# Two layers with attention, recurrence and a convolution: the z gates as plain float32 products queued behind the scores, the modulation split into single steps

## Chip, cores and metric

One NeuronCore of a Trainium2 chip runs the whole program. The metric is the device time of one execution in microseconds (us), the median of several runs. In the text PE is TensorE, DVE VectorE, ACT ScalarE, POOL GpSimd and SP the queue that issues most loads.

## What is computed

256 tokens of width 1024 pass two equal layers ("first block"), then one block of latent attention and a matrix LSTM, and then a layer of experts (256 gathers of rows). The change lies in the two layers, and in the modulation vectors that the second block uses. Cut to that, the reference is:

```python
for l in range(2):
    h = rms_norm(x, norm_g[l])
    proj = h @ w_in[l]
    (q, k_c, v_c, k_s, v_s, k_w, v_w, g_lin, z_nsa, u_lru, z_lru, glu_a, glu_b, z_conv) = split(proj)
    ...
    y_nsa = nsa_attention(...)      # compressed, selected and window branch
    y_lru = rg_lru(u_lru, ...)      # linear recurrence over the tokens
    y_conv = conformer_conv(...)    # 31 taps, layer norm, product with w_pw2
    mixed = concatenate([y_nsa * silu(z_nsa), y_lru * silu(z_lru), y_conv * silu(z_conv)])
    x = x + mixed @ w_out[l]

mod_lat = silu(c) @ w_ada + b_ada       # second block: shifts, scales and gates
mod_ctx = silu(c_ctx) @ w_ada + b_ada
```

The z gates are 12 of the 128-wide column blocks of the first product. The modulation is a product of two vectors with a 1024 x 6144 matrix; its sixth part is summed elsewhere and stays.

## The kernel before

Tokens lie along the free dimension (256), features along the 128 partitions. A weight tile is 128 x 1024 float32 (512 KB): eight 128 x 128 blocks that make 128 output features. `wload` (L310) issues its load on SP into one of five raw buffers, `wsplit` (L318) makes a high part of it on ACT (copy to the reduced type fp32r) and a low part on DVE (the difference), and `mm3` (L350) multiplies with three products a block: high by high, low by high, high by low, 24 products of 256 columns for a tile. The normalised input is held split in the same way (`hh`, `hl`).

A layer runs: norm, products of the column blocks (`proj2`, L572), attention (`attend`, L764) with other work between its steps, and the out-projection (`woa`, 8 tiles; `wob`, 4 tiles). `attend` yields after each score: 14 pieces per layer (for two blocks of 128 queries, the selected and window branches and then the compressed one). The string ORDER (L237) says what is put after each yield: letters A to F are pairs of z tiles (`zpair`, L755), digits the gates of the recurrence, c the compression of keys, s the scan, w, p, q the product behind the convolution, x, y, z its norm. `conv_norm` starts with a sum over the four convolution outputs (the first product of line 412 in the tail), and the taps of the convolution are DVE instructions that are put in behind splits.

A list scheduler orders the instructions on each engine: `at(us)` gives what follows a priority, loads and splits get an earlier one, and `tc.issue_after(ins)` puts an instruction behind another on its engine. So a z pair stands where its priority puts it, and its tiles fill the time between scores.

The modulation (`modulation`, `part`, L958) has five parts of eight tiles, each tile with four small products (32 x 256) of line 963 into one PSUM buffer `c`, from two raw buffers (`wm`). `hook` (L1665) calls three parts in layer 0 and two in layer 1, at fixed priorities P["mt"]. A "step" below is one tile with its four products.

```python
def zpair(i):
    acc = proj2(20 + i)
    th = mk(b1, [128, 2, T], tag="tmp2", bufs=2)
```

Of the kernel before, what the change touches and what calls it, by code (L numbers as in the profile page):

```python
# [9 lines left out]
F32R = mybir.dt.float32r  # L10
# [219 lines left out]

P = dict(np=5, glu=14, kv=35, kk=40, q=41, cmp=46, cmpd=5, w1n=62, cv0=32, cvd=35, att=57, attd=5, mix=137, woa=131, ln=145, pw2=160, wob=138, mod=5, ll=25000, sl=6000, nm=3, mt=(62, 80, 170, 243, 270), sp=29, L0=10, L1=196, S=369, B=500, cx=125, h1=2, h2=6, X=16, lri=37, lnk=7, tp=2, tq=0, ta=0, ml=40, mld=2.6, rt=36, g0=-32, ga=104, gb=161, gc=157)

# [4 lines left out]
def program(tc, A, dbg=lambda *a: None, stop=99):  # L241
# [11 lines left out]
        return p.tile(list(shape), dt, name=f"{tag}_{cnt[0]}", tag=tag, **kw)  # L253

    def mm(out, lhsT, rhs, start, stop):
        pe.matmul(out, lhsT, rhs, start=start, stop=stop)  # L256

    def tr(out, in_, ident):
        pe.transpose(out, in_, ident)  # L259
# [90 lines left out]
    def mm3(out, pairs, first=True, last=True, late=False):  # L350

        n = len(pairs)
        for i, (ah, al, bh, bl) in enumerate(pairs):
            mm(out, ah, bh, first and i == 0, False)
            if late:
                mm(out, al, bh, False, False)
            else:
                mm(out, ah, bl, False, False)
                mm(out, al, bh, False, last and i == n - 1)
        if late:  # L360
            for i, (ah, al, bh, bl) in enumerate(pairs):
                mm(out, ah, bl, False, last and i == n - 1)

    def rsqrt(p, v, shape, tag, bufs=2):

# [20 lines left out]
    def psum(tag, shape):  # L386
        if tag == "acc":
            turn[1] = (turn[1] + 1) % 3
            tag = "acx" if turn[1] == 0 else "acc"
        return mk(ps, shape, tag=tag, bufs=PB[tag])  # L390
# [55 lines left out]
    hh = mk(cp, [128, 8, T], F32R, tag="hh")  # L446
    hl = mk(cp, [128, 8, T], F32R, tag="hl")

    def norm_apply(p, src, gain, shift=None, hi=None, lo=None, bc=None):
        if bc is None:  # L450
            bc = norm_rstd(p, [src[:, k] for k in range(8)], D)
        g6 = None if hi is not None else slot("g6", 2048).rearrange("p (k t) -> p k t", k=8)
        if hi is None:
            hi, lo = hh, hl
        p0 = tc.cur_priority
        for k in range(0, 8, 2):
            tc.cur_priority = p0
            t = mk(p, [128, 2, T], tag="tmp2", bufs=2) if g6 is None else g6[:, k:k + 2]
            for q in range(2):
                scaled[:] = [dve.scalar_tensor_tensor(t[:, q], src[:, k + q], gain[:, k + q:k + q + 1], bc, op0=mul, op1=mul)]  # L460
            if shift is None:
                last = act.activation(hi[:, k:k + 2], t, AF.Copy)
                if g6 is not None:
                    tc.cur_priority = p0 + 4000
                tt(lo[:, k:k + 2], t, hi[:, k:k + 2].bitcast(F32), sub)
            else:
                for q in range(k, k + 2):
                    last = act.activation(hi[:, q], t[:, q - k], AF.Identity, bias=shift[:, q:q + 1])  # L468
                if g6 is not None:
                    tc.cur_priority = p0 + 4000  # L470
                for q in range(k, k + 2):
                    stt(lo[:, q], t[:, q - k], shift[:, q:q + 1], hi[:, q].bitcast(F32), add, sub)
        tc.cur_priority = p0
        return last
# [5 lines left out]
    def slot(tag, n, dt=F32, bufs=1):  # L480

        return mk(b1, [128, SLOTS[tag]], dt, tag=tag, bufs=bufs)[:, 0:n]
# [80 lines left out]
    def layer(l, L, hook=lambda n: None):  # L563
# [8 lines left out]
        def proj2(i, t=None):  # L572

            acc = psum("acc", [128, 2, T])
            for q in range(2):
                if t is not None:
                    at(L + t + 2.6 * q)
                wh, wl = wsplit(A["w1"][l, i + q], [128, 8, 128])
                mm3(acc[:, q], [(wh[:, k], wl[:, k], hh[:, k], hl[:, k]) for k in range(8)], late=i == 0)
            if t is not None:  # L580
                at(L + t + 5.2)
            return acc
# [170 lines left out]
        gzc = slot("gz4", 1024).rearrange("p (i t) -> p i t", i=4)  # L753

        def zpair(i):  # L755
            acc = proj2(20 + i)
            th = mk(b1, [128, 2, T], tag="tmp2", bufs=2)
            act.activation(th, acc, AF.Tanh, scale=0.5)
            stt(gz[:, i:i + 2] if i < 8 else gzc[:, i - 8:i - 6], th, 1.0, acc, add, mul)


        onat = []

        def attend(b):  # L764
            bs = slice(b * 128, b * 128 + 128)
# [13 lines left out]
            for bi in (1, 2):  # L779
                step = 2 - b  # L780
                for jj in range(0, 4, step):
                    js = list(range(jj, jj + step))
                    sps = psum("s", [128, step, 2, nk])
                    for ji, j in enumerate(js):
                        mm(sps[:, ji], qT[:, j, bs], kz[:, bi - 1, :, 0:nk], True, False)
                        mm(sps[:, ji, :, nk - 128:], identb, cmaskb[:, None, :].broadcast_to([128, 2, 128]), False, True)
                    nh = 2 * step
                    s2 = sps.rearrange("p a g k -> p (a g) k")
                    mx = mk(b1, [128, 4], tag="mxs", bufs=4)
# [23 lines left out]

            cps = psum("s", [128, 4, 2, 15])
            for j in range(4):
                mm(cps[:, j], qT[:, j, bs], kcz, True, True)
            c8 = cps.rearrange("p j g n -> p (j g) n")
            sc = mk(b1, [128, 8, 15], tag="sc", bufs=1)
            cm = C("cmpm")[:, 16 * b:16 * b + 15]
# [21 lines left out]
            onat.append(oT)  # L841


        g6 = slot("g6", 2048, F32R).rearrange("p (w i t) -> p w i t", w=2, i=4)
        mch, mcl = g6[:, 0], g6[:, 1]

        def pick(i):
            return (hh, hl, i) if i < 8 else (mch, mcl, i - 8)

        def msplit(i, src):  # L850
            h, lo, j = pick(i)
# [42 lines left out]
                     q=lambda: conv_proj(2, pw))  # L894
        for i in range(4):
            steps[str(i)] = lambda i=i: lru_gates(i)
        for i, c in enumerate("ABCDEF"):
            steps[c] = lambda i=i: zpair(2 * i)
        for c in "xyz":
            steps[c] = lambda: next(cn)  # L900
        order = ORDER[l].split(",")
# [18 lines left out]
        for n in range(0, 8, 2):  # L920
            acc = psum("acc", [128, 2, T])
            for q in range(2):
                at(L + P["woa"] + 2.6 * (n + q))
                wh, wl = wsplit(A["woa"][l, n + q], [128, 8, 128])
                mm3(acc[:, q], [(wh[:, k], wl[:, k], hh[:, k], hl[:, k]) for k in (4, 5, 6, 7, 0, 1, 2, 3)])
            stt(XT[:, n:n + 2], acc, 0.5, XT[:, n:n + 2], mul, add)
            for c in order.pop(0):
                steps[c]()

        for n2 in range(4):  # L930
            at(L + P["wob"] + 2.6 * n2)
            wh, wl = wsplit(A["wob"][l, n2], [128, 4, 256])
            acc = psum("acc", [128, 2, T])
            for q in range(2):
                s = slice(q * 128, q * 128 + 128)
                mm3(acc[:, q], [(wh[:, k, s], wl[:, k, s], mch[:, k], mcl[:, k]) for k in range(4)])
            stt(XT[:, n2 * 2:n2 * 2 + 2], acc, 0.5, XT[:, n2 * 2:n2 * 2 + 2], mul, add)
# [6 lines left out]
    def modulation():  # L944
# [3 lines left out]
        def prep():  # L948
# [6 lines left out]
            ts(s2, s2, 0.5, None, mul)  # L955
            act.activation(sc0, sc[:, :, 0], AF.Copy)

        def part(m):  # L958
            acc = psum("c", [128, 256])
            for k in range(8):  # L960
                w = wload(A["wada"][m, k], [128, 4, 256], "wm", NWM, b1)
                for j in range(4):
                    pe.matmul(acc[32 * j:32 * j + 32], sc[:, k], w[:, j], start=k == 0, stop=k == 7,  # L963
                              tile_position=(0, 32 * j))
            rows = slot("ang", 256)
            act.activation(rows, acc, AF.Copy)
            tp = psum("c", [128, 2, 128])
            for q in range(2):
                tr(tp[:, q], rows[:, q * 128:q * 128 + 128], ident)
            src = tp.rearrange("p q (j w) -> p j q w", w=32)[:, :, :, 0:2]  # L970
            tt(modt[:, m * 8:m * 8 + 8].rearrange("p (j q) w -> p j q w", q=2), src,
               P2("bada")[:, m * 8:m * 8 + 8].rearrange("p (j q) -> p j q", q=2)[:, :, :, None].broadcast_to([128, 4, 2, 2]), add)
            if m == 1:
                for nm, w in (("lat", 0), ("ctx", 1)):
                    mg[nm] = mk(cp, [128, 8], tag="mg" + nm)
                    stt(mg[nm], modt[:, 8:16, w], 1.0, P2("g1"), add, mul)
            if m == 4:
                mg["pr"] = mk(cp, [128, 8], tag="mgpr")
                stt(mg["pr"], modt[:, 32:40, 0], 1.0, P2("g2"), add, mul)

        return [prep] + [lambda m=m: part(m) for m in (1, 0, 2, 4, 3)[:int(P["np"])]]

    def modsum(acc, m, k):

# [5 lines left out]
            stt(acc, w, s, acc, mul, add)  # L990

    def modparts():
        for m in (4, 3)[int(P["np"]) - 3:]:
            acc = mk(b1, [128, 1024], tag="wm", bufs=NWM)
            for k in range(8):
                modsum(acc, m, k)
# [661 lines left out]
            pass  # L1658
        pp.release()

    steps = modulation()
    at(P["mod"])
    steps.pop(0)()

    def hook(n, l):  # L1665
        if n == 0:
            if l == 1:
                next(two)
            return
        for i in range(min(int(P["nm"]), len(steps)) if l == 0 else len(steps)):  # L1670
            at(P["mt"][int(P["np"]) - len(steps)])
            steps.pop(0)()

    layer(0, P["L0"], lambda n: hook(n, 0))
    two = second(P["L1"] + P["cx"], P["S"])
# [18 lines left out]
```

## Time and profile before

| | |
|---|---|
| median of 3 runs | 1381.29 us (1377.42 to 1384.13) |
| the profiled execution | 1384.02 us |
| its span in the trace | 1382.2 us |
| mean granted clock of TensorE | 0.946 |
| PE, DVE, ACT busy | 1193.9, 991.6, 530.5 us |
| float32 weight splits, DVE | 142 in 171.4 us |
| gathers of the experts, chain | 27% of the span |

A row of the trace gives the start (us from the span's start), the busy time, the engine, the line of the kernel, the operation with the tile it writes and the tiles it reads, and in brackets how long the engine had been idle and what ended that. A float32 product of 128 or more columns is two hardware instructions, so that x4 is two products of the program; a split product is one. Layer 0 takes the time from about 16 to 248 us, layer 1 from there to about 500.

### The profile page before, as it was taken

The numbers are of one execution on the slowest core, as the hardware profiler recorded it, in microseconds if no ns is written. First come the engines' busy times: TensorE is split into PE (matmuls) and PEld (weight loads), VectorE is DVE, ScalarE is ACT, GpSimd is POOL, SyncE is SP. The second block draws the span as 40 slices with busy tenths as digits, with TensorE's granted clock in tenths as the row PEclk, the third lists the DMA queues.
The fourth block names the chain that finished last, engine by engine and source line by source line (L and its number), as shares of the span: only waits on it lengthen the run. The fifth ranks groups of instructions, "written<-read, shape, count | busy, mean of one in ns | idle before, by whom it ended". The sixth has DMA issues, their size and how long they took to land.

```text
span 1382.2 us, 17743 instructions
## 1 busy us (share of the span) xinstructions
PE 1193.9 (86%) x5972; PEld 775.5 (56%) x5972; DVE 991.6 (72%) x2440; ACT 530.5 (38%) x1136; POOL 296.2 (21%) x279
## 2 busy tenths in 40 slices
PE   6999889899979999999898877778887878778776
PEld 5987659698947986658794323343333333323332
DVE  6898865599988676566678776777766767676554
ACT  5635643344755555554543212222212222212211
POOL 0000000000000000000024444434453444444441
PEclk9999999899999999999999999999899999999999
DMA  8587454547413442401479999999999999999996
GB/s 321 196 282 274 158 183 168 197 158 264 137 41 100 153 130 83 146 16 46 138 313 387 422 422 421 421 409 384 421 414 422 421 419 397 424 421 398 421 422 263
DMA packets 71340, 387.50 MB, mean 280 GB/s; under 512 B 8402, under 2 KB 9426, under 8 KB 38227
## 3 DMA queue, kind: packets, MB, share of 16 engines
q0 software_dynamic: 36864, 268.45, 47.1%
q1 hardware_dynamic: 34386, 117.93, 24.7%
q8 instruction: 48, 0.79, 0.2%
q14 instruction: 42, 0.34, 0.1%
HBM read 385.30 MB, written 1.05 MB: 280 GB/s over the span
## 4 chain that ended last, share of the span: by engine, by line
PE 48%; DMA 30%; DVE 8%; issue 7%; POOL 4%; ACT 2%; POOLq 0%; DVEq 0%; SPq 0%; ACTq 0%
DMA G<-uv,eix 27%; PE acc L256 22%; PE acx L256 11%; PE s L256 5%; POOL G L1583 4%; DVE G L1586 4%; DMA wm<-wada 2%; PE c L963 2%; PE t L256 2%; PE o L256 2%; PE s L412 1%; PE t L259 1%; PE c L256 1%; PE o L811 1%; PE o L645 1%
## 5 line engine op out<-in xcount | busy, mean ns | idle before, releaser
L1586 DVE SCALAR_TENSOR_TENSOR G<-G,hn 128x1024 f32<-128x1024 f32 x256 | 313.4, 1224 | 177.3 <-DMA G<-uv,eix 170.2
L1583 POOL DMA_INDIRECT G<-uv,eix x256 | 288.7, 1128 | 438.8 <-PE acx L256 140.6
L268 DVE TENSOR_TENSOR wl<-w,wh 128x1024 fp32r<-128x1024 f32 (+2 forms) x142 | 171.4, 1209 | 69.8 <-ACT wh L323 68.3
L323 ACT ACTIVATE wh<-w 128x1024 fp32r<-128x1024 f32 (+2 forms) x142 | 148.5, 1048 | 188.1 <-PE acc L256 115.7
L256 PE MATMUL t<-G,dg 128*128 128x512 f32 x256 | 146.5, 656 | 70.1 <-ACT dg L1599 70.1
L256 PE MATMUL c<-G,dg 128*128 128x512 f32 x256 | 148.1, 663 | 62.4 <-ACT dg L1599 62.4
L256 PE MATMUL acc<-hh,wh 128*128 128x256 f32 x608 | 178.5, 297 | 7.8 <-ACT hh L468 3.6
L256 PE MATMUL acc<-hh,wl 128*128 128x256 f32 x608 | 176.8, 293 | 2.7 <-DVE wl L268 2.0
L256 PE MATMUL acc<-hl,wh 128*128 128x256 f32 x608 | 166.5, 287 | 1.2 <-DVE hl L268 1.1
L1599 ACT ACTIVATE dg<-cst,w 128x128 f32<-128x128 f32 x256 | 89.4, 394 | 149.1 <-PE o L256 64.4
L256 PE MATMUL acx<-G,dg 128*128 128x512 f32 x256 | 143.1, 643 | 0.0
L256 PE MATMUL o<-G,dg 128*128 128x512 f32 x256 | 141.2, 635 | 0.0
L1590 ACT ACTIVATE s<-s 128x4 f32<-128x4 f32 (+1 forms) x66 | 13.5, 205 | 325.2 <-DVE G L1586 325.2
L256 PEld LDWEIGHTS t<-G,dg 128*128 128x128 f32 x256 | 50.2, 206 | 149.9 <-ACT dg L1599 96.0
L256 PEld LDWEIGHTS acc<-hh,wh 128*128 128x128 f32 x608 | 119.3, 197 | 16.2 <-issue 4.7
L256 PEld LDWEIGHTS c<-G,dg 128*128 128x128 f32 x256 | 50.5, 209 | 135.1 <-ACT dg L1599 83.3
L256 PEld LDWEIGHTS acc<-hh,wl 128*128 128x128 f32 x608 | 119.7, 197 | 7.1 <-DVE wl L268 2.9
L256 PEld LDWEIGHTS acc<-hl,wh 128*128 128x128 f32 x608 | 113.8, 193 | 5.8 <-issue 3.2
L262 DVE SCALAR_TENSOR_TENSOR g<-lu,pb,g 128x256 f32<-128x256 f32 x264 | 115.0, 476 | 0.2
L256 PEld LDWEIGHTS o<-G,dg 128*128 128x128 f32 x256 | 53.2, 208 | 69.9 <-issue 69.9
L256 PEld LDWEIGHTS acx<-G,dg 128*128 128x128 f32 x256 | 52.7, 206 | 69.0 <-issue 69.0
L1054 POOL MEMSET lu<- 128x16 f32 x1 | 0.4, 447 | 401.9 <-DVE g L262 401.9
(512 smaller groups left out, 1947.6 us busy)
## 6 DMA issues: line engine op xcount, KB each, us to landing
w<-w SPq DMA_DIRECT2D x64, 512.0 KB, 4.6
wm<-wada SPq DMA_DIRECT2D x40, 512.0 KB, 4.5
wa<-cw SPq DMA_DIRECT2D x16, 512.0 KB, 5.1
w<-woa SPq DMA_DIRECT2D x16, 512.0 KB, 3.5
w<-wpq SPq DMA_DIRECT2D x16, 512.0 KB, 3.5
w<-w2t SPq DMA_DIRECT2D x12, 512.0 KB, 3.5
w<-wob SPq DMA_DIRECT2D x8, 512.0 KB, 4.6
w<-w2v SPq DMA_DIRECT2D x8, 512.0 KB, 3.8
```

The lines of the kernel that those rows point to most:

```text
L256: pe.matmul(out, lhsT, rhs, start=start, stop=stop)
L259: pe.transpose(out, in_, ident)
L262: (e or dve).scalar_tensor_tensor(out, a, s, b, op0=op0, op1=op1)
L268: return (e or dve).tensor_tensor(out, a, b, op=op)
L323: act.activation(hi, w, AF.Copy)
L412: pe.matmul(acc[j:j + 32], ones[:, 0:32], sq[:, q] if square else srcs[i + q], start=i + q < 4, stop=i + q >= n - 4, tile_position=(0, j))
L645: pe.matmul(hps[32 * j:32 * j + 32], blk[:, q4 * 4 + j], w[:, j], start=q4 == 0, stop=q4 == 3, tile_position=(0, 32 * j))
L811: pe.matmul(ops[gs, jj:jj + step], vsw[kb][:, bi - 1, gs], p4[:, :, g, kb], start=bi == 1 and kb == 0 and jj == 0, stop=False, tile_positi ...
L963: pe.matmul(acc[32 * j:32 * j + 32], sc[:, k], w[:, j], start=k == 0, stop=k == 7, tile_position=(0, 32 * j))
L1583: pool.indirect_dma_start(out=G, out_offset=None, in_=A["uv"], in_offset=bass.IndirectOffsetOnAxis(ap=eix[b][:, h, k:k + 1], axis=0))
L1586: dot = dve.scalar_tensor_tensor(G[:, 0:D], G[:, 0:D], 1.0, hn[b], op0=mul, op1=mul, accum_out=s[:, j:j + 1])
L1599: act.activation(dg, ident, AF.Copy, scale=w[:, j:j + 1])
```

## The change

1. `zpair` doesn't split its weight tiles. It multiplies the raw tile with the unsplit normalised input (`whole[0]`, which stays in its buffer `g6`) in full float32: 8 products for a tile.
2. Each z pair is queued on TensorE behind the last score product of its step (`held`, with `asked[0]`).
3. The modulation is cut into 45 pieces (40 steps and five ends of a part). `fill` puts the next one behind the last product of a weight tile, for two tiles of three, in `proj2`, the z tiles and `woa`. Two modulation tiles are loaded at the start, and each step issues the next load.

```diff
+    modq, tiles_done = [], [0]
+
+    def fill(end):
+        tiles_done[0] += 1
+        if modq and tiles_done[0] % 3:
+            p = tc.cur_priority
+            with tc.issue_after(end.ins):
+                modq.pop(0)()
+            tc.cur_priority = p
...
+        whole[:] = [g6]
...
-                mm3(acc[:, q], [(wh[:, k], wl[:, k], hh[:, k], hl[:, k]) for k in range(8)], late=i == 0)
+                fill(mm3(acc[:, q], [(wh[:, k], wl[:, k], hh[:, k], hl[:, k]) for k in range(8)], late=i == 0))
...
         def zpair(i):
-            acc = proj2(20 + i)
+
+            acc = psum("acc", [128, 2, T])
+            for q in range(2):
+                w = wload(A["w1"][l, 20 + i + q], [128, 8, 128])
+                for k in range(8):
+                    end = mm(acc[:, q], w[:, k], whole[0][:, k], k == 0, k == 7)
+                fill(end)
...
+        def held(i):
+            with tc.issue_after(asked[0].ins):
+                zpair(i)
+
         for i, c in enumerate("ABCDEF"):
-            steps[c] = lambda i=i: zpair(2 * i)
+            steps[c] = lambda i=i: held(2 * i)
...
-                mm3(acc[:, q], [(wh[:, k], wl[:, k], hh[:, k], hl[:, k]) for k in (4, 5, 6, 7, 0, 1, 2, 3)])
+                fill(mm3(acc[:, q], [(wh[:, k], wl[:, k], hh[:, k], hl[:, k]) for k in (4, 5, 6, 7, 0, 1, 2, 3)]))
...
+        def load():
+            if order:
+                m, k = order.pop(0)
+                loaded.append(wload(A["wada"][m, k], [128, 4, 256], "wm", NWM, b1))
...
+        def products(m, k):
+            if k == 0:
+                accs[m] = psum("c", [128, 256])
+            w = loaded.pop(0)
+            for j in range(4):
+                pe.matmul(accs[m][32 * j:32 * j + 32], sc[:, k], w[:, j], start=k == 0, stop=k == 7,
+                          tile_position=(0, 32 * j))
+            load()
...
+    at(P["L0"] + P["glu"])
+    load()
+    load()
+    modq.extend(steps)
 
     def hook(n, l):
-        if n == 0:
-            if l == 1:
-                next(two)
-            return
-        for i in range(min(int(P["nm"]), len(steps)) if l == 0 else len(steps)):
-            at(P["mt"][int(P["np"]) - len(steps)])
-            steps.pop(0)()
+        if n == 0 and l == 1:
+            next(two)
```

The asked[0] of the diff is set by the score products in `attend`. Where the order moves:

On TensorE at the start of the attention of layer 0, before (s is a score or a compressed key, acc from hh, hl and wh, wl a split z tile, o from wa the compression, line 645):

```order
L645 MATMUL o_901<-wa_908,blk_89 32x256 x4
L256 MATMUL acx_1000<-wh_1055,hl_82 128x280
L256 MATMUL s_994<-hid_144_892,cw_109_646 128x30
L256 MATMUL s_1273<-g_10_86 128x256
L256 MATMUL s_1273<-cmaskb_76,identb_74 128x256
L256 MATMUL acc_1360<-hh_81,wl_1365 128x256
L256 MATMUL acc_1360<-hh_81,wh_1363 128x256
L256 MATMUL acc_1360<-hl_82,wh_1363 128x256
```

The same place after the change (line 660 is the compression, line 1004 the modulation, acc from g and w a z tile):

```order
L256 MATMUL s_1197<-g_10_86 128x256
L256 MATMUL s_1197<-cmaskb_76,identb_74 128x256
L660 MATMUL o_983<-wa_996,blk_89 32x256 x4
L256 MATMUL s_1088<-hid_163_974,cw_120_699 128x30
L660 MATMUL o_983<-wa_1002,blk_89 32x256 x4
L256 MATMUL t_1180<-cst_62,rows_1008 128x30 x2
L256 MATMUL s_1226<-g_10_86 128x256
L256 MATMUL s_1250<-g_201_1190,g_96_526 128x256 x2
L256 MATMUL s_1264<-g_10_86 128x256
L256 MATMUL acc_1284<-g_37_163,w_1285 128x256 x8
L256 MATMUL acc_1284<-g_37_163,w_1295 128x256 x8
L1004 MATMUL c_776<-wm_1047,silc_103 32x256 x4
```

Before, the products of the first z tile stand around the first score. After, two halves of the compression and three scores stand ahead of any z product.

On TensorE between the layers, before (t from dg turns the norm's factors, s from cst sums over the features):

```order
L963 MATMUL c_3634<-wm_3647,silc_103 32x256 x4
L963 MATMUL c_3634<-wm_3653,silc_103 32x256 x4
L412 MATMUL s_2674<-tmp_435_2685,cst_62 32x256 x2
L412 MATMUL s_2674<-tmp_436_2690,cst_62 32x256 x2
L256 MATMUL s_2697<-cst_62,tmp_2695 128x1 x2
L963 MATMUL c_3634<-wm_3659,silc_103 32x256 x4
L963 MATMUL c_3634<-wm_3665,silc_103 32x256 x4
L256 MATMUL t_2716<-dg_2717,cst_62 128x128
L256 MATMUL t_2716<-dg_2720,cst_62 128x128
L963 MATMUL c_3634<-wm_3671,silc_103 32x256 x4
```

After:

```order
L256 MATMUL acc_2412<-g_355_1994,wl_2410 128x256
L424 MATMUL s_2438<-tmp_413_2449,cst_62 32x256 x2
L424 MATMUL s_2438<-tmp_414_2454,cst_62 32x256 x2
L256 MATMUL s_2461<-cst_62,tmp_2459 128x1 x2
L256 MATMUL t_2480<-dg_2481,cst_62 128x128
L256 MATMUL t_2480<-dg_2484,cst_62 128x128
L256 MATMUL acc_2504<-hh_81,wh_2507 128x256
```

The modulation steps have left this place; the first of them in layer 1 stands behind the first weight tile.

## Rows read from the trace of the kernel before

**Rows 1.** The chain of waits over the whole span, by line.

```profile
by line: DMA G<-uv,eix 27.2%; PE acc L256 22.0%; PE acx L256 10.5%; issue 7.3%; PE s L256 5.1%; POOL G L1583 4.2%; DVE G L1586 3.6%; DMA wm<-wada 2.0%; PE c L963 1.7%; PE t L256 1.7%; PE o L256 1.5%; PE s L412 1.0%; PE t L259 0.9%; PE c L25
```

**Rows 2.** Windows: length, busy us (instructions) of PE, PEld, DVE, ACT, POOL; clock, DMA.

```profile
99.00:159.00 60.00, 60.00 (x472) 48.87 (x468) 52.08 (x132) 35.48 (x85) 0.00 (x0) 1.00 0.64 224
159.00:204.00 45.00, 37.51 (x305) 19.38 (x304) 34.34 (x113) 21.91 (x58) 0.00 (x0) 0.90 0.60 206
...
385.00:433.00 48.00, 36.92 (x234) 22.40 (x235) 38.68 (x126) 28.43 (x75) 0.45 (x1) 0.93 0.13 42
```

**Rows 3.** The chain of waits in order of time: start, us, what.

```profile
60.89 2.88 PE acc L256 x24
```

**Rows 4.** The chain from 159 to 204 us: by line, and one piece.

```profile
by line: DMA wm<-wada 40.1%; PE c L963 18.9%; PE s L256 15.5%; PE t L259 6.6%; PE o L811 6.5%; PE o L256 4.3%; PE s L412 2.5%; ACT pr L794 2.3%; PE c L259 1.9%; ACT ang L966 0.9%; issue 0.8%
...
188.33 0.57 PE c L963 x8
```

**Rows 5.** Waits of PE from 99 to 181 us: total, times, longest.

```profile
PE s L256 <- ACT pr L794: 2.5, 2, 1.3
PE c L963 <- DMA wm<-wada: 1.9, 3, 1.1
```

**Rows 6.** Windows of line 963 alone: length, busy PE and PEld, clock, DMA.

```profile
159.00:204.00 45.00, 11.31 (x128) 2.93 (x128) 0.90 0.60 206
...
248.00:262.00 14.00, 4.94 (x48) 1.22 (x48) 0.68 0.70 244
```

**Rows 7.** Timeline of PE inside a z tile and in the convolution's product.

```profile
122.82 0.28 PE L256 MATMUL acx<-hh,wl 128*128 128x256 f32 x1
...
123.82 0.28 PE L256 MATMUL acx<-hl,wh 128*128 128x256 f32 x1
...
206.87 1.03 PE L256 MATMUL acc<-g,wa 128*128 128x256 f32 x4
207.73 1.03 PE L256 MATMUL acx<-g,wa 128*128 128x256 f32 x4
```

**Rows 8.** The page: groups (busy us, mean ns), loads (KB, us to landing).

```profile
L268 DVE TENSOR_TENSOR wl<-w,wh 128x1024 fp32r<-128x1024 f32 (+2 forms) x142 | 171.4, 1209 | 69.8 <-ACT wh L323 68.3
L323 ACT ACTIVATE wh<-w 128x1024 fp32r<-128x1024 f32 (+2 forms) x142 | 148.5, 1048 | 188.1 <-PE acc L256 115.7
...
w<-w SPq DMA_DIRECT2D x64, 512.0 KB, 4.6
...
wa<-cw SPq DMA_DIRECT2D x16, 512.0 KB, 5.1
```

**Rows 9.** Timeline of PE: first scores, convolution sums (L412), out-projections, one idle.

```profile
99.80 0.68 PE L256 MATMUL s<-g 128*128 128x256 f32 x2
...
180.86 0.62 PE L412 MATMUL s<-g,cst 128*32 128x256 f32 x2
...
211.00 0.47 PE L256 MATMUL acc<-hh,wh 128*128 128x256 f32 x1
...
333.33 0.60 PE L256 MATMUL s<-g 128*128 128x256 f32 x2
...
390.51 0.45 PE L259 MATMUL t<-cst,pr 128*128 128x128 f32 x1 [4.41 <-DVE pr L265]
...
411.86 0.64 PE L412 MATMUL s<-g,cst 128*32 128x256 f32 x8
...
433.68 0.48 PE L256 MATMUL acc<-hh,wh 128*128 128x256 f32 x2
```

**Rows 10.** Timeline between the layers, DVE and PE.

```profile
253.81 0.48 DVE L265 TENSOR_SCALAR dg<-cst,ny 128x128 f32<-128x128 f32 x2
...
256.41 1.22 PE L256 MATMUL t<-dg,cst 128*128 128x128 f32 x4
...
261.37 1.08 PE L963 MATMUL c<-wm,silc 128*32 128x256 f32 x8
```

**Rows 11.** A window of 6 us behind the idle of rows 9.

```profile
391.00:397.00 6.00, 6.00 (x15) 2.28 (x14) 6.00 (x16) 2.85 (x7) 0.00 (x0) 0.54 0.00 1
```

More of the change, by code (lines that the diff above doesn't have):

```diff
@@ L229, in pack @@
     return {k: np.ascontiguousarray(v) for k, v in o.items()}
-P = dict(np=5, glu=14, kv=35, kk=40, q=41, cmp=46, cmpd=5, w1n=62, cv0=32, cvd=35, att=57, attd=5, mix=137, woa=131, ln=145, pw2=160, wob=138, mod=5, ll=25000, sl=6000, nm=3, mt=(62, 80, 170, 243, 270), sp=29, L0=10, L1=196, S=369, B=500, cx=125, h1=2, h2=6, X=16, lri=37, lnk=7, tp=2, tq=0, ta=0, ml=40, mld=2.6, rt=36, g0=-32, ga=104, gb=161, gc=157)
+P = dict(glu=14, kv=35, kk=40, q=41, cmp=46, cmpd=5, w1n=62, cv0=32, cvd=35, att=57, attd=5, mix=137, woa=131, ln=145, pw2=160, wob=138, mod=5, ll=25000, sl=6000, sp=29, L0=10, L1=196, S=369, B=500, cx=125, h1=2, h2=6, X=16, lri=37, lnk=7, tp=2, tq=0, ta=0, ml=40, mld=2.6, rt=36, g0=-32, ga=104, gb=161, gc=157)
 ORDER = [",0,C1c,E2,,3s,B,,DF,Aw,x,,y,zp,q,,,", "C,0,c1,2F3w,,D,E,sB,,,,Ax,y,z,p,q,,"]
@@ L255, in mm @@
     def mm(out, lhsT, rhs, start, stop):
-        pe.matmul(out, lhsT, rhs, start=start, stop=stop)
+        return pe.matmul(out, lhsT, rhs, start=start, stop=stop)
     def tr(out, in_, ident):
@@ L358, in mm3 @@
                 mm(out, ah, bl, False, False)
-                mm(out, al, bh, False, last and i == n - 1)
+                end = mm(out, al, bh, False, last and i == n - 1)
         if late:
             for i, (ah, al, bh, bl) in enumerate(pairs):
-                mm(out, ah, bl, False, last and i == n - 1)
+                end = mm(out, ah, bl, False, last and i == n - 1)
+        return end
+    modq, tiles_done = [], [0]
[6 more added lines that the diff above has]
+            tc.cur_priority = p
     def rsqrt(p, v, shape, tag, bufs=2):
@@ L447, in program @@
     hl = mk(cp, [128, 8, T], F32R, tag="hl")
+    whole = []
     def norm_apply(p, src, gain, shift=None, hi=None, lo=None, bc=None):
@@ L762, in layer @@
         onat = []
+        asked = [None]
         def attend(b):
@@ L785, in attend @@
                         mm(sps[:, ji], qT[:, j, bs], kz[:, bi - 1, :, 0:nk], True, False)
-                        mm(sps[:, ji, :, nk - 128:], identb, cmaskb[:, None, :].broadcast_to([128, 2, 128]), False, True)
+                        asked[0] = mm(sps[:, ji, :, nk - 128:], identb, cmaskb[:, None, :].broadcast_to([128, 2, 128]), False, True)
                     nh = 2 * step
@@ L815, in attend @@
             for j in range(4):
-                mm(cps[:, j], qT[:, j, bs], kcz, True, True)
+                asked[0] = mm(cps[:, j], qT[:, j, bs], kcz, True, True)
             c8 = cps.rearrange("p j g n -> p (j g) n")
@@ L841, in attend @@
             onat.append(oT)
-        g6 = slot("g6", 2048, F32R).rearrange("p (w i t) -> p w i t", w=2, i=4)
-        mch, mcl = g6[:, 0], g6[:, 1]
+        mc = []
         def pick(i):
-            return (hh, hl, i) if i < 8 else (mch, mcl, i - 8)
+            if i < 8:
+                return hh, hl, i
+            if not mc:
+                g6 = slot("g6", 2048, F32R).rearrange("p (w i t) -> p w i t", w=2, i=4)
+                mc.extend((g6[:, 0], g6[:, 1]))
+            return mc[0], mc[1], i - 8
         def msplit(i, src):
@@ L932, in layer @@
             wh, wl = wsplit(A["wob"][l, n2], [128, 4, 256])
+            mch, mcl = mc
             acc = psum("acc", [128, 2, T])
@@ L956, in prep @@
             act.activation(sc0, sc[:, :, 0], AF.Copy)
-        def part(m):
[L959 to L964, printed above, removed]
+        loaded = []
+        order = [(m, k) for m in (1, 0, 2, 4, 3) for k in range(8)]
+        def load():
+            if order:
+                m, k = order.pop(0)
+                loaded.append(wload(A["wada"][m, k], [128, 4, 256], "wm", NWM, b1))
+        accs = {}
+        def products(m, k):
[6 more added lines that the diff above has]
+            load()
+        def part(m):
+            acc = accs[m]
             rows = slot("ang", 256)
@@ L979, in part @@
                 stt(mg["pr"], modt[:, 32:40, 0], 1.0, P2("g2"), add, mul)
-        return [prep] + [lambda m=m: part(m) for m in (1, 0, 2, 4, 3)[:int(P["np"])]]
+        steps = []
+        for m in (1, 0, 2, 4, 3):
+            steps += [lambda m=m, k=k: products(m, k) for k in range(8)] + [lambda m=m: part(m)]
+        return prep, load, steps
     def modsum(acc, m, k):
@@ L992, in modparts @@
     def modparts():
-        for m in (4, 3)[int(P["np"]) - 3:]:
+        for m in ():
             acc = mk(b1, [128, 1024], tag="wm", bufs=NWM)
@@ L1659, in peer @@
         pp.release()
-    steps = modulation()
+    prep, load, steps = modulation()
     at(P["mod"])
-    steps.pop(0)()
-    def hook(n, l):
-        if n == 0:
-            if l == 1:
-                next(two)
-            return
-        for i in range(min(int(P["nm"]), len(steps)) if l == 0 else len(steps)):
-            at(P["mt"][int(P["np"]) - len(steps)])
-            steps.pop(0)()
+    prep()
+    at(P["L0"] + P["glu"])
+    load()
+    load()
+    modq.extend(steps)
+    def hook(n, l):
+        if n == 0 and l == 1:
+            next(two)
     layer(0, P["L0"], lambda n: hook(n, 0))
```

## The prediction

> **What bounds the kernel now.** I read first where the end comes from. The chain of waits [rows 1] ends in 27.2% gathers of expert rows, and these start only when the routing is ready. Behind the out-projection of layer 1 the two instruction orders are the same on TensorE, so whatever the two layers gain or lose before about 433 us arrives at the end one for one. The question is those 433 us alone.
>
> Then the windows of the attention stage of layer 0 [rows 2]: from 99 to 159 us TensorE is busy 60.00 of 60.00 us. In the tail behind it, 159 to 204, it is busy 37.51 of 45; in the tail of layer 1, 385 to 433, 36.92 of 48. So each stage is a stretch bound by TensorE, then a tail of dependent steps in which it waits. A busy row alone doesn't say that TensorE works at its pace, so I looked at the pace: 24 split products of a weight tile take 2.88 us [rows 3], 0.12 each, without a hole.
>
> Two views tell what the tail of layer 0 waits for. The chain of that tail [rows 4] is 40.1% DMA of modulation tiles (wm from wada) and 18.9% their products; the waits up to 181 us [rows 5] give 2.5 us of TensorE behind exponentials and 1.9 behind those DMAs. The windows of the modulation's line [rows 6] show where it runs: 11.31 us of products stand in the tail of layer 0, 4.94 us in the 14 us between the layers, at a granted clock of 0.68. By count of the order that is 8 steps (one tile, four products) before the first score, 8 beside the z tiles, 16 in the tail, 2 in the out-projection, 6 between the layers.
>
> **The change part by part.**
>
> *z gates.* 24 tiles (12 a layer) lose 24 products at 0.12 and get 8 in full float32. In the convolution's product a row of four hardware instructions, which are two float32 products of the same size, starts 0.86 us before the next (206.87 to 207.73 [rows 7]). So one product costs 0.43 and a tile 8 x 0.43 = 3.44 against 2.88: +0.56 a tile, **+6.7 us in each layer**, all in stretches where TensorE is the bound. Removed beside it: 24 splits of 1.21 us on VectorE and 24 copies of 1.05 us on ScalarE [rows 8], which lie under TensorE's work; I pay nothing for them in the forecast, and the third case prices them. The raw tile stays until its products have run, with five buffers and 4.6 us to land [rows 8] against 3.44 us a tile: nothing, by that cover. The whole normalised input must live until z is done; its buffer is next wanted after the convolution's norm (180.86 and 411.86 [rows 9]) and both z parts lie before them: nothing.
>
> *Modulation.* The same 40 steps, one by one. A step inside a tile sets its next products back by 0.76 us (122.82 to 123.82 [rows 7], where two products would have taken 0.24), one in the tail took 0.57 [rows 4]; I take 0.65, the middle. New places: 13 before the first score of layer 0 (5 more: **+3.2**), 7 in that stage (before 24), 4 in its out-projection (before 2: **+1.3**), none between the layers, 12 before the first score of layer 1 and with them some eleven products of the narrow tile that now stand ahead of it (12 x 0.65 + 11 x 0.12 = **+9.1**), 4 in that stage.
>
> *Layer 0, first score to the convolution's sum.* 81.1 us now (99.80 to 180.86 [rows 9]), about 4.6 of it the waits of rows 5, so 76.5 of work. Less 24 steps, plus 7, plus z (−15.6 + 4.6 + 6.7), plus two scores of about 1 us that move ahead of the sum: 74.3. To this come new waits. In the new order three scores stand nearly bare before the first z tile, since z is queued behind the score of its step; a compression weight is loaded only once its buffer has been read, and such a load takes 5.1 us [rows 8]; the third score wants a PSUM buffer that the exponentials free, as they held scores for 2.5 us [rows 5]. I take 2.7 + 2.6 there and 2.7 in the tail, 8 in all (bounds 2 and 16): 82.4, **+1.3**.
>
> *Layer 0, tail.* From the sum to the out-projection's steady run takes 30.1 us (180.86 to 211) and in layer 1, the same chain with no modulation in it, 21.8 (411.86 to 433.68) [rows 9]. Take 8.3 away, and put back two groups of float32 products of 0.86 that layer 1 had already run: **−6.6**.
>
> *Between the layers.* dg is ready at 254.29, the transposes that want it start at 256.41 behind two modulation steps, and two more steps stand behind it, at 1.08 us each (the second at 261.37) [rows 10], partly under the wait for hh: 2.1 + 1.9 = **−4** (bounds 2 and 6).
>
> *Layer 1, first score to the sum.* 78.5 now (333.33 to 411.86). Waits are about 9 us (the 4.41 at 390.51 [rows 9] the longest), and some 3 are lost at half clock after it [rows 11]; 66.5 is work. Plus 6.7 of z and 4 x 0.65, less the 1.3 that moved ahead: 74.5, and 4 of the 9 us of waits, since VectorE is relieved there: 78.5, **0** (bounds −4 and +6).
>
> *Layer 1, tail.* 24 products of the first out-projection tile now stand ahead of the mean: 24 x 0.12 = **+2.9**.
>
> Queues: the modulation loads are issued two ahead and each waits for the product before it on SP; behind them stand the z loads, but a step comes in two tiles of three, so the queue is not held longer than a tile. POOL has nothing of this. **Sum: 3.2 + 1.3 − 6.6 + 1.3 − 4 + 9.1 + 0 + 2.9 = +7.2**, say +7. The bounds together give −2 to +15. The profiled execution took 1384.0; the median of the runs is 1381.3, so a median after is **1388**.
>
> **A rule against the reading.** The Trainium skill ("Trainium Kernel Development and Optimization", Performance Expectations) warns that matmul busy time is a bad metric for the distance to the bound, because matmuls are pipelined. If so here, a full row of windows would hide slack, z's 13.4 us would cost nothing, and the sum would be −6. The pace of rows 3 speaks against it: the products follow each other at 0.12 us.
>
> **The rivals.**
> *Slower by more: bare scores cool TensorE.* In layer 1 TensorE idled 4.41 us at 390.51 [rows 9] and then ran the 6 us from 391 on at a mean granted clock of 0.54 [rows 11], next to the lower of its two levels, 1.2 of 2.4 GHz; that cost 6 x 0.46, some 3 us. The change makes two or three such bare places, before the first z tiles of layer 0 and at a score that waits for exponentials. If the compression weight takes its 5.1 us rather than 2.7, and the clock falls three times, 3 x 3 and a little over 1: +10 over the sum, +17, 1398 (1392 to 1405). It decides where the bare waits come to the size of that 4.41. The Trainium skill ("TensorE: Matmul & The Clock Gate", HAM oscillation) says the same of gaps in general, that the work behind one starts cold; whether it falls here, only the new trace shows. Against it: z tiles follow soon, and waits of 1 to 2 us in the tail cost less.
> *Faster: the splits were the bound.* VectorE and ScalarE lose 24 x 1.21 and 24 x 1.05 us [rows 8] just where the score's maxima, the exponentials and the convolution's taps run. Then the taps end early, the waits that I left in layer 0 (8) shrink to 2 and those of layer 1 (4) to none, and each tail falls from 21.8 to about 18 (−8), the steps cost their 0.57 (−2): −20 on the sum, −13, so 1368 (1361 to 1377). For it: the tail of layer 1 waits for VectorE and ScalarE. Against: in the 60 us of rows 2 VectorE was busy 52.08 and TensorE never waited.
> *The change does not do what it says:* the modulation tiles are not there when their place comes, and the stalls move with them. Then no tail gains and the new steps wait: within 0 to +10.
>
> **How the numbers follow.** Forecast +7 (1379 to 1396): 0.54. Slower rival: 0.20. Faster rival: 0.23. Not as it says: 0.03. The range 1369 to 1401 holds the forecast's, two thirds of the slower one's, half of the faster one's. A measurement of this kernel tells about 0.5%, 6.9 us, from no change. Faster than 1374.4: four fifths of the faster rival, 0.19. Slower than 1388.2: nearly all of the slower rival and half of the forecast, 0.46. The rest, 0.35.
>
> **What would show it.** Right: no wait for wada on TensorE in the tail of layer 0, the tail there near 23.5 us, z tiles at 3.4 us, the first score of layer 1 later after its stage's start by 9, the same time from there to its sum. Wrong: z tiles under 3 us, or a first score to sum well under 75 us in both layers (the splits were the bound), or over 90 with a low granted clock (the bare scores). What would break the whole: a shift before 433 us that does not arrive at the end.

## The result, and the profile after

The changed kernel takes 1421.12 us (median of 4, 1417.86 to 1423.32) against 1379.36 for the kernel before beside it: ratio 1.0297, 95% interval 1.0258 to 1.0336. It is slower by 42 us, where 1388 (1369 to 1401) had been forecast. The spans of the two profiled executions differ by 38.5 us (1420.7 and 1382.2).

I first aligned the two traces at four events that both have: the sum over the convolution's outputs in layer 0, the first product of layer 1, the same sum in layer 1, and the out-projection's steady start. Between them lie four stretches; PE's columns for them in the trace after are (length, busy PE, PEld, DVE, ACT, POOL, clock, DMA):

```profile
16.00:200.10 184.10, 176.98 (x1132) 131.62 (x1133) 136.09 (x323) 82.35 (x170) 0.00 (x0) 0.96 0.58 201
200.10:273.11 73.01, 63.68 (x473) 52.36 (x472) 43.00 (x103) 28.45 (x55) 0.00 (x0) 0.96 0.42 144
273.11:441.76 168.65, 163.32 (x1092) 128.80 (x1092) 126.89 (x300) 73.20 (x161) 0.13 (x1) 0.97 0.49 173
441.76:470.57 28.81, 25.94 (x165) 16.33 (x164) 13.34 (x48) 12.41 (x33) 0.00 (x0) 0.82 0.19 64
```

And before:

```profile
16.00:180.86 164.86, 157.92 (x1236) 128.05 (x1236) 146.47 (x331) 90.29 (x177) 0.00 (x0) 0.98 0.68 239
180.86:260.00 79.14, 71.58 (x587) 56.70 (x586) 44.07 (x109) 30.90 (x59) 0.00 (x0) 0.93 0.57 196
260.00:411.86 151.86, 143.95 (x1094) 125.18 (x1090) 137.23 (x305) 83.22 (x167) 0.45 (x1) 0.97 0.44 147
411.86:433.68 21.82, 18.64 (x141) 12.17 (x140) 14.91 (x54) 13.51 (x37) 0.00 (x0) 1.00 0.18 61
```

Stretch A (to the sum of layer 0) grew by 19.2 us, B shrank by 6.1, C (layer 1 to its sum) grew by 16.8 and D by 7.0; what follows differs by 1.6. So the shift before 433 us did arrive at the end nearly one for one (36.9 of 38.5). The forecast by the same stretches was +4.5, −9.3, +9.1 and +2.9. A and C hold most of the error.

These rows of stretch A in the trace after (PE alone) show what is new:

```profile
107.15 1.08 PE L660 MATMUL o<-wa,blk 128*32 128x256 f32 x8 [3.16 <-DMA wa<-cw]
...
116.36 1.22 PE L256 MATMUL s<-g 128*128 128x256 f32 x2 [0.93 <-ACT g L747]
...
126.68 0.64 PE L1004 MATMUL c<-wm,silc 128*32 128x256 f32 x8
127.25 0.70 PE L256 MATMUL s<-g,g 128*128 128x256 f32 x2
...
148.66 3.62 PE L256 MATMUL acx<-g,w 128*128 128x256 f32 x16
152.21 0.62 PE L1004 MATMUL c<-wm,silc 128*32 128x256 f32 x2
152.76 0.44 PE L259 MATMUL t<-cst,pc 128*128 128x128 f32 x2
153.03 0.60 PE L256 MATMUL acx<-g,w 128*128 128x256 f32 x2
153.56 0.62 PE L1004 MATMUL c<-wm,silc 128*32 128x256 f32 x2
154.11 1.13 PE L256 MATMUL acx<-g,w 128*128 128x256 f32 x4
155.17 0.62 PE L1004 MATMUL c<-wm,silc 128*32 128x256 f32 x2
155.72 0.70 PE L256 MATMUL acx<-g,w 128*128 128x256 f32 x2
156.35 0.62 PE L1004 MATMUL c<-wm,silc 128*32 128x256 f32 x2
```

Three things stand here. A z tile takes 148.66 to 152.21, 3.55 with the switch behind it, as priced. The bare waits before the first z tile are there, the longest 3.16 us. And the modulation steps have two forms. At 126.68 all four products of a step stand together (x8) and take 0.57 us until the next instruction. At 152.21 they are cut apart: one product (x2), a z product, another product. Each then takes 0.55 alone (152.21 to 152.76, 153.56 to 154.11), and a z product between two of them 0.63 (155.72 to 156.35) rather than 0.43. A step cut like that costs some 2.2 us of its own, and its z products some 0.2 us each on top.

The windows of the modulation's tiles alone say how much that is (length, busy PE, clock, DMA). After:

```profile
102.00:200.00 98.00, 14.27 (x56) 0.93 0.41 138
...
355.00:441.00 86.00, 6.23 (x32) 0.96 0.36 121
```

And before, from the first score of layer 0 to the sum:

```profile
99.80:180.86 81.06, 12.53 (x128) 0.96 0.64 224
```

7 steps (x56, six of them cut) take 14.27 us, 2.0 each; before, 16 steps (x128) took 12.53 in that stage, 0.8 each. The x8 and x2 of the rows are hardware instructions. In the code `fill` gives the step the same priority as the next z tile, and the scheduler let the two alternate; the first experiment changes that priority alone.

The half clock came as well, in the 15 us from 105, in which the wait before 107.15 (the first row) ends, and in the tail of layer 1:

```profile
105.00:120.00 15.00, 11.36 (x42) 7.03 (x43) 10.99 (x40) 5.38 (x23) 0.00 (x0) 0.54 0.32 111
...
452.00:468.00 16.00, 13.31 (x68) 7.68 (x63) 8.92 (x38) 6.64 (x20) 0.00 (x0) 0.68 0.24 82
```

An estimate of the loss is the busy time times what is missing of full clock: 11.36 x 0.46, 5.2 us, and 13.31 x 0.32, 4.3 us.

### The profile page after: what moved, and what is told of

Same layout as the page of the kernel before. It is cut to its first block, busy times and chain, and to the rows that moved or that the text cites. A ratio compares the mean times of both kernels' runs of the same rounds, so it can differ in the third digit from the quotient of the medians.

```text
span 1420.7 us, 17256 instructions
## 1 busy us (share of the span) xinstructions
PE 1228.8 (86%) x5780; PEld 782.2 (55%) x5780; DVE 969.1 (68%) x2416; ACT 507.7 (36%) x1112; POOL 297.7 (21%) x279
## 4 chain that ended last, share of the span: by engine, by line
PE 51%; DMA 22%; issue 10%; DVE 7%; POOL 6%; ACT 3%; POOLq 0%; DVEq 0%; SPq 0%; ACTq 0%
PE acc L256 23%; DMA G<-uv,eix 22%; PE acx L256 11%; PE s L256 6%; POOL G L1631 6%; DVE G L1634 3%; PE c L1004 2%; PE o L256 2%; PE t L256 2%; PE s L424 1%; PE c L256 1%; PE t L259 1%; PE o L833 1%; PE o L660 1%; ACT wh L323 1%
## 5 line engine op out<-in xcount | busy, mean ns | idle before, releaser
L256 PE MATMUL c<-G,dg 128*128 128x512 f32 x256 | 144.8, 649 | 65.4 <-ACT dg L1647 65.2
L268 DVE TENSOR_TENSOR wl<-w,wh 128x1024 fp32r<-128x1024 f32 (+2 forms) x118 | 142.2, 1207 | 70.1 <-ACT wh L323 69.4
L323 ACT ACTIVATE wh<-w 128x1024 fp32r<-128x1024 f32 (+2 forms) x118 | 123.2, 1045 | 175.7 <-PE acc L256 111.6
L256 PE MATMUL acc<-hh,wh 128*128 128x256 f32 x480 | 144.5, 304 | 12.3 <-ACT wh L323 5.4
L256 PE MATMUL acc<-hh,wl 128*128 128x256 f32 x480 | 141.0, 297 | 1.3 <-DVE wl L268 1.3
L256 PE MATMUL acc<-hl,wh 128*128 128x256 f32 x480 | 130.0, 288 | 0.7 <-DVE hl L268 0.7
L256 PEld LDWEIGHTS acc<-hh,wh 128*128 128x128 f32 x480 | 96.2, 201 | 22.2 <-ACT wh L323 7.0
L256 PEld LDWEIGHTS acc<-hh,wl 128*128 128x128 f32 x480 | 96.2, 201 | 4.2 <-DVE wl L268 1.6
L256 PEld LDWEIGHTS acc<-hl,wh 128*128 128x128 f32 x480 | 90.0, 195 | 2.5 <-issue 1.4
```

The source lines that it names most:

```text
L256: return pe.matmul(out, lhsT, rhs, start=start, stop=stop)
L268: return (e or dve).tensor_tensor(out, a, b, op=op)
L323: act.activation(hi, w, AF.Copy)
```

## The experiments

Eleven kernels in twelve runs. I split the change into three parts: float32 z, the queueing behind the scores, and the single steps; and the steps again into where they stand and whether their four products stay together. Ratios are to the kernel before, timed beside each. Its median was 1379.4 us beside the change and 1384.1 to 1386.1 beside the experiments, so that times of different sessions differ by up to 7 us for that alone; where times and ratios disagree, the ratios count.

**Steps kept whole.** In the changed kernel the step gets an earlier priority than the next tile:

```diff
             p = tc.cur_priority
+            tc.cur_priority = p - 100
             with tc.issue_after(end.ins):
```

> The changed kernel, but the four products of a modulation step get an earlier priority than the next weight tile, so that 36 of 40 steps stand whole on TensorE (30 of 40 in the changed kernel, where most of the others have a z product between each two of the four). Theory A (four products side by side take about 0.57 us together, but 0.55 us each when a z product stands between them, as the trace of the changed kernel has it): the steps inside the z tiles get 1.6 to 1.9 us cheaper each, about 7 of them: 11 to 14 us less than the changed kernel's 1421, so 1407 to 1410. Theory B (the bare scores and the half clock behind them cost the time): nothing of that is touched, 1418 to 1423.

Measured: 1402.1 us, 1.0126 (1.0085 to 1.0167). That is 19 us under the change by the times and 24 by the ratios, more than the 11 to 14 of theory A. Both kernels have the same 1132 instructions on PE in stretch A; with whole steps they are

```profile
16.00:186.46 170.46, 163.47 (x1132) 129.60 (x1132) 135.10 (x322) 81.39 (x169) 0.00 (x0) 0.97 0.62 215
```

busy 163.47 instead of 176.98 us, and the stretch is 13.6 shorter. The seven steps:

```profile
102.00:200.00 98.00, 6.31 (x56) 0.98 0.41 143
```

0.9 each, 8.0 us less in all (four are whole now, three still have one product apart). The rest of the 13.6 is, by estimate, the z products that no longer stand between, some 0.2 us each, and some 2.3 of clock (184.1 x 0.04 less 170.5 x 0.03), which may be chance. Theory A is shown.

**No queueing.** The changed kernel without `held`:

```diff
-            with tc.issue_after(asked[0].ins):
-                zpair(i)
+            zpair(i)
```

> The changed kernel without the queueing of z pairs behind their step's score. Theory B: the z tiles fill the waits at the first scores again, the idle of 5 us and the half clock of window 99 to 159 (0.89) go in layer 0, and about as much in layer 1 (0.93): 12 to 18 us less, 1403 to 1409. Theory A: the split steps stay, at most 5 us less, 1416 to 1421.

1398.24 us, 1.0081 (1.0046 to 1.0116): 23 us less than the change by the times and 30 by the ratios, more than theory B's 18. The steps are still cut (12.41 us for 6 in the stage of layer 0). So both theories hold. The clock goes with the queue in every kernel: from 99 to 130 us TensorE idled 4.3 to 6.3 us at a granted clock of 0.78 to 0.94 in the five kernels that have the queue, and at most 0.7 us at 1.00 in all the others.

**Both edits.**

> The changed kernel with whole modulation steps and without the queueing of z pairs: both edits of the first two runs together. They took 19 and 23 us off alone. If they are two causes (steps cut apart, bare scores), most of both goes: the kernel without queueing spends 12.4 us on 6 steps in the stage of layer 0 where 4 would do, and 3.7 on 2 in layer 1, so 8 to 11 us less than its 1398: 1387 to 1390. If the two edits only removed the same loss (the queueing being what cuts the steps apart), nothing more comes: 1396 to 1400.

1385.39 us, 1.0018 (0.9994 to 1.0041). Two causes that overlap in part: 1.0297 falls by 0.0171 and 0.0216 apart, 0.0387 in sum, and by 0.0279 together. Whole steps are worth 0.0171 with the queue and 0.0063 without it. PE in stretches A, C and D:

```profile
16.00:176.23 160.23, 158.57 (x1108) 126.41 (x1108) 134.47 (x321) 80.15 (x167) 0.00 (x0) 0.98 0.65 228
...
251.03:411.60 160.57, 160.57 (x1116) 130.16 (x1116) 128.19 (x298) 72.01 (x157) 0.13 (x1) 0.98 0.53 185
411.60:435.19 23.59, 20.46 (x137) 12.69 (x136) 13.99 (x51) 13.62 (x37) 0.00 (x0) 0.93 0.17 57
```

In C PE is busy for the whole stretch. With the queueing and whole steps it idled 5.1 us there (165.46 − 160.33), 7.0 in A and D took 28.1 instead of 23.6.

**Float32 z alone**, on the kernel before:

```diff
-            acc = proj2(20 + i)
...
+                w = wload(A["w1"][l, 20 + i + q], [128, 8, 128])
+                for k in range(8):
+                    end = mm(acc[:, q], w[:, k], whole[0][:, k], k == 0, k == 7)
```

> The kernel before with z gates in full float32 alone, modulation and queueing as before. If TensorE's pace is the bound beside the z tiles, 24 x 0.58 us come on top: 1393. If the splits of VectorE and ScalarE were the bound, 1370 to 1379. If the z products cut apart the modulation steps as they do in the changed kernel, over 1395.

1377.43 us, 0.9937 (0.9915 to 0.9958). It is *faster* than before, if by little. Run again:

> z gates in full float32 alone, once more and with more rounds, as the measure for the next two: 0.992 to 0.996 of before.

0.9971 (0.9949 to 0.9993), a little less gain than I expected, the intervals just overlapping. The 13.4 us that I had put on TensorE don't appear in the time:

```profile
16.00:173.49 157.49, 155.46 (x1087) 126.48 (x1087) 134.29 (x321) 78.78 (x163) 0.00 (x0) 0.98 0.64 225
...
253.89:406.41 152.52, 152.52 (x1050) 128.02 (x1050) 125.87 (x297) 71.79 (x156) 0.13 (x1) 0.98 0.49 168
```

PE's idle in A and C was 6.9 + 7.9 before and is 2.0 + 0.0 here, 12.8 us less. Its busy time there grew by 6.1 only (301.87 to 307.98), with 0.8 more of modulation in it; why by less than 13.4 was not tried. On VectorE the last tap of the convolution in layer 0, which its sum needs, starts at 180.4 us before, just ahead of the sum (180.86), and at 129.0 here, 44 us ahead of it.

To see whether the gain is the relief of the two engines or only another order, the next kernel keeps their work:

```diff
                 w = wload(A["w1"][l, 20 + i + q], [128, 8, 128])
...
+                hi = mk(wp, [128, 8, 128], F32R, tag="wh", bufs=NSP)
+                act.activation(hi, w, AF.Copy)
+                lo = mk(wp, [128, 8, 128], F32R, tag="wl", bufs=NSP)
+                ins = tt(lo, w, hi.bitcast(F32), sub)
...
```

> The same kernel, but ScalarE and VectorE still split every z tile, 24 copies and 24 differences whose results nobody reads; the products stay full float32 of the raw tile. If the gain of float32 z comes from the relief of these two engines (TensorE idle fell from 14.8 us in the two layers' stretches to 2.0), it goes: TensorE's 13.9 us stay and the idle returns, ratio 1.000 to 1.010. If the gain comes from the other order of the work alone: 0.992 to 0.997.

1390.67 us, 1.0062 (1.0041 to 1.0082). The gain is gone, and more than half of PE's idle is back:

```profile
16.00:176.80 160.80, 157.76 (x1109) 126.98 (x1109) 145.81 (x332) 89.68 (x175) 0.00 (x0) 0.98 0.66 231
...
255.69:415.18 159.49, 153.88 (x1021) 128.14 (x1017) 134.70 (x300) 81.42 (x165) 0.13 (x1) 0.96 0.44 150
```

3.0 + 5.6 us of 14.8. The relief of VectorE and ScalarE is what pays for the float32 products. In layer 0 one reservation stays: the taps are tied to the splits there (two behind each) and came back with them, so work and order moved together. In layer 1 no tap is tied to a split, and stretch C alone is 7.0 us longer than without the splits (159.49 against 152.52).

**The queueing without the steps**, with float32 z and with split z:

```diff
...
-            steps[c] = lambda i=i: zpair(2 * i)
+            steps[c] = lambda i=i: held(2 * i)
```

> z gates in full float32 and queued behind the scores, modulation as before. Beside the kernel with float32 z alone (0.994 of before) it differs by the queueing alone. If bare scores cost by themselves: 8 to 20 us more than that, ratio 1.000 to 1.008. If the queueing hurts only by cutting the modulation's steps apart, which the old order does little: within 4 us of it, ratio 0.991 to 0.997.

> The kernel before with nothing but the queueing of its (split) z pairs behind the scores. If bare scores cost by themselves: 6 to 15 us more than before, ratio 1.004 to 1.011. If not: 0.997 to 1.003. It may even gain, if scores that come earlier shorten the tails: that would be under 0.997.

With float32 z 1.0074 (1.0038 to 1.0109): 1.0 to 1.4% over float32 z alone, so the queue costs by itself, with the old steps too. What stands bare there is something else, though: the longest wait in layer 0 (4.42 us, before 109.74) is for a modulation tile, where the changed kernel's 3.16 is for a compression weight. With split z 1.0033 (1.0008 to 1.0058), between the two cases that I had written, nearer to none.

**The steps alone**, cut and whole, with split z and no queueing:

> The kernel before with the modulation in single steps behind weight tiles alone; z gates split and not queued. Gain by the tail of layer 0 (about 7 us) and the gap between the layers (4 us), loss by 12 more steps ahead of the scores of layer 1 and 5 of layer 0 (11 us) : 1376 to 1384 by theory B, where nothing else is lost. By theory A, steps cut apart by split products of z cost 4 x 0.55 us each here too: 1388 to 1396.

> The single modulation steps alone, as in the run with only steps (ratio 1.012), but whole: 29 of 40 or more stand whole in both, yet the others here lose one product at most. In that run 7 steps in the stage of layer 0 took 14.1 us, 2.0 each. Theory A: 7 to 9 us less there and 1 to 2 in layer 1, ratio 1.004 to 1.007, and what is left is the 12 steps that moved ahead of layer 1's scores, 16 us dearer now, against the shorter tail. If cutting apart does not matter with split z tiles: 1.010 to 1.013.

1.0117 (1.0079 to 1.0155) and 1.0044 (1.0016 to 1.0073). Theory A again: split z products cut the steps just as well, at 0.7%; the first of the two runs is dearer than even theory A had it (1388 to 1396 us, measured 1401.78). Whole steps are still not a gain. Against the kernel before A and B are 4.2 us shorter, but C, where 10.1 us more of steps stand, is 7.8 longer and D 2.3.

**The change with split z.**

> The changed kernel with split z tiles (fp32r, 24 products) in place of float32; queueing and single steps as in the change. If float32 is what hurts in the change: 10 to 14 us less than 1421, ratio 1.018 to 1.022. If steps that are cut apart cost about 2 us each whatever product cuts them, and the queueing costs as much as in the others, it stays near the change: 1.022 to 1.032.

1.0218 (1.0178 to 1.0258), at the border of the two cases. Its stretches A and C:

```profile
16.00:192.54 176.54, 167.55 (x1225) 131.60 (x1225) 145.31 (x331) 92.45 (x181) 0.00 (x0) 0.98 0.60 207
...
268.30:438.05 169.75, 161.20 (x1200) 131.55 (x1200) 137.51 (x309) 83.34 (x172) 0.13 (x1) 0.95 0.50 169
```

Float32 makes the queued change dearer by some 0.8% (1.0297 against 1.0218) and the kernel before cheaper by 0.3 to 0.6%. Queued, TensorE's busy time in A and C grows by 11.5 us with float32 and its idle falls by 5.2 only; without the queue and with the old steps it grew by 6.1 and the idle fell by 12.8. With the queue and the old steps the difference is 0.4%, not clear of the noise.

The parts and their combinations in one table; idle is length less PE's busy time in stretches A and C, worked out from windows as those above.

| kernel | z | queued | steps | ratio | idle A + C, us | length of D, us |
|---|---|---|---|---|---|---|
| before | split | no | old | 1 | 6.9 + 7.9 | 21.8 |
| z alone, twice | float32 | no | old | 0.994, 0.997 | 2.0 + 0.0, 2.4 + 0.0 | 24.3, 22.1 |
| queue alone | split | yes | old | 1.003 | 8.0 + 7.9 | 28.8 |
| z and queue | float32 | yes | old | 1.007 | 6.8 + 6.1 | 28.4 |
| steps alone | split | no | cut | 1.012 | 8.1 + 3.9 | 23.5 |
| steps alone | split | no | whole | 1.004 | 8.1 + 7.0 | 24.1 |
| steps, queue | split | yes | cut | 1.022 | 9.0 + 8.6 | 28.1 |
| z and steps | float32 | no | cut | 1.008 | 1.8 + 0.0 | 23.4 |
| z and steps | float32 | no | whole | 1.002 | 1.7 + 0.0 | 23.6 |
| all, whole | float32 | yes | whole | 1.013 | 7.0 + 5.1 | 28.1 |
| **the change** | float32 | yes | cut | 1.030 | 7.1 + 5.3 | 28.8 |

**A version from what was found**: float32 z, not queued, whole steps, and the steps in other places:

```diff
-        if modq and tiles_done[0] % 3:
+        if tiles_done[0] % 3 == 0:
+            slip(end)
...
+                    if b == 1:
+                        slip(end)
```

> A version meant to beat both: z in full float32 and not queued, modulation steps whole, one behind every third weight tile, one behind each of the 8 late attention steps of a layer (where TensorE waits) and the last behind layer 1's out-projection. Against the kernel with whole steps and no queueing (1.002) some 16 steps move from full stretches, 0.7 to 1.0 us each, into holes of the tails, where they cost 0 to 0.6 if their tiles have landed: ratio 0.990 to 0.997. If the loads, two in flight at 4.5 us each, come too late for 8 steps in a row, TensorE waits for wada there again: 0.998 to 1.005.

1378.27 us, 0.9958 (0.9936 to 0.9980), as expected: faster than both kernels, as fast as float32 z alone within the intervals. It reaches the out-projection of layer 1 at 425.7 us, 8 before [rows 9], and the end is 5 earlier; some 3 go behind that, where its last steps stand. Float32 z alone is the simplest version that beats both.

## Why the prediction was wrong

*z gates, +6.7 us in each layer.* The tile's price was right (3.46 in the chain of the changed kernel against 3.44). "I pay nothing for" the splits was wrong. They lay under TensorE's work only in the 60 us of [rows 2]; in the stages as a whole TensorE waited 14.8 us, mostly behind what these two engines did, and without the splits and without the queue 13 of that go. That was the mechanism of my faster rival. The rule on busy time that stood beside the forecast put z's 13.4 us at nothing as well, and for z alone nothing is what came, but for the whole change its −6 was further off than mine.

*Modulation, 0.65 a step.* This step failed most. Both my rows (0.76 and 0.57) show four products that stand together. The order after the change had them one by one between z products, and I priced them alike. In the stage of layer 0, 7 steps, six of them cut, took 14.27 us where 4.6 were in the sum, and keeping the steps whole took 1.7% off the program (24 us by the ratios). For steps that stand together the price was right: the 12 before the first score of layer 1 took 8.26 us, 0.69 each. The Trainium skill ("TensorEngine Tiling (Array Packing)", Key Properties) says why such a difference is to be expected: column tiles work independently, so four run side by side, and changing the tiling mode drains the engine. The trace agrees: 0.57 us for four together, 0.55 us for each one alone; no row shows the drain by itself.

*Layer 0, first score to the sum, +1.3.* It was +16.4 (97.4 us from 102.66 to 200.10, against 81.1). Before and after:

```profile
99.80:180.86 81.06, 76.55 (x581) 55.70 (x579) 71.00 (x185) 46.19 (x111) 0.00 (x0) 0.96 0.64 224
...
102.66:200.10 97.44, 92.44 (x438) 58.67 (x438) 54.49 (x151) 38.02 (x100) 0.00 (x0) 0.93 0.41 139
```

One error is in the sum itself. I took 24 steps out of this stage, but 16 stood there (x128 in the window of the modulation above); the other 8 ran behind the sum, and the −8.3 of the tail already took them out. Counted once, the term is 5.2 us more, +6.5, and the whole forecast +12.4. The waits that I put there at 8 us came to 5.0 (97.44 less 92.44). What is left is 9.7 us of cut steps (14.27 instead of 4.6), the z products between them, and the half clock from 107 to 120 us, which the forecast left to the slower rival.

*Layer 0's tail and the gap.* −6.6 + 1.3 − 4 = −9.3 against −6.1 measured. The tail was right: no wait for wada is left there, and up to the steady run of the out-projection it fell from 30.1 to 22.7 us (200.10 to 222.81), −7.4. The gap from the last product of the out-projection to the first of layer 1 fell by 3.0 (12.1 to 9.1): without the steps TensorE waits 2.6 us for dg there. The out-projection itself grew by 4.3 where 1.3 was forecast; its four steps explain 1.7 of that (3.17 us against 1.46 for two), and the rest is open.

*Layer 1.* +9.1 before the first score: right (355.77 − 273.11 = 82.7 against 73.3, +9.3). First score to the sum: 0 forecast, +7.5 measured (86.0). 3.6 of that are the steps (6.23 us instead of 2.6), and the idle did not shrink to 4 but to 5.3. The tail: +2.9 forecast, +7.0 measured. The 24 products are there and take 3.0 us, as forecast. TensorE waits no longer than before (28.81 − 25.94 = 2.9 us against 3.2), but the clock is 0.82 where it was 1.00, which is 4.7 us by its busy time. All kernels of the table with the queue have 28 to 29 us there, all without it 22 to 24. Why the clock falls in this tail, with waits that the kernel before has too, stays open.

*The rivals.* The slower one, bare scores that cool TensorE, happened, and its sign too (over 90 us at a lower clock), though its 1398 lacked the cut steps. The queue's price with float32 z is 1.0 to 1.4% with the old steps, 1.1% with whole and 2.2% with cut ones; with split z, which has no relief to lose, it is 0.3% with the old and 1.0% with cut ones. The faster one happened in part in the kernel with z alone: the waits fell to 2.0 and 0.0 as it had them, but the tail of layer 1 took 24.3 and 22.1 us, not 18. What I missed is that the change's parts work against each other: the queue removes what float32 z gains.

## What to carry to other kernels

When pieces are put one by one between others, read in the new order whether instructions that ran side by side still stand together; a price read from a group is not the price of its members. Beside a full engine, what another engine's work costs is the full engine's waits over the whole stage, not over its fullest stretch. When a stage is split at an event, count on which side of it each piece stands, or it is taken out twice. And a piece of work that fills holes should not be queued behind the thing whose wait it fills.

## What was not expected of the hardware

Four 32-column float32 products of 256 columns took 0.57 us together and 0.55 each between products that use all columns, 3.9 times as much in all; a full product between two of them took 0.63 instead of 0.43. And with the wait of 3.16 us before 107.15 the granted clock was 0.54 over the 15 us from 105; the same kernel with whole steps waited 1.87 and 1.58 us at that place, with products between, and had 0.89 over the same 15 us. Why the two executions differ there was not tried.
